# Weight sums with plus signs only, added up by DMAs in DRAM from the heads on; eight of eleven down steps by seven products

## The chip, the cores and the metric

The kernel runs on one core of one Trainium2 chip. The metric is the device time of one execution in microseconds (us); for the kernel before, the median of three runs is 1213.9 us (1212.75 to 1214.02). PE is TensorE (its weight loads are PEld), DVE is VectorE, ACT is ScalarE, POOL is GpSimd, and SP is SyncE, which here only issues DMAs.

## The reference, and what is computed

One layer of a hybrid decoder on 16 meta tokens and 256 tokens, with a model width of 2048, all in float32:

```
u = rmsnorm(h, norm_mix);  proj = u @ w_in           # 2048 -> q, k, v, gates of 8 retention and 4 mLSTM heads
mix = concatenate([ret, hm]) @ w_out                 # the heads' outputs, normed and gated
h = h + mix
u = rmsnorm(h, norm_ffn)
up = causal_dwconv(u @ w_up, ffn_conv_w, ffn_conv_b) # 2048 -> 2 x 5632, convolution over 3 tokens
gate, val = split(up)
h = h + (silu(gate) * val) @ w_down                  # 5632 -> 2048
return rmsnorm(h, norm_final)[:, 16:]
```

## The kernel before, in words

**Products.** Every product of float32 matrices is made of three matmuls: a value is split into a high part (a cast to the type fp32r, by ACT) and a low part (value less high part, by DVE), and high x high, high x low and low x high are summed in PSUM. For weights this is `load_w`: SP loads 512 KB into a buffer `wraw` (four buffers, L118), ACT casts it into `whi` (L121), DVE subtracts into `wlo` (L123; five buffers each). `project` and `half_tile` then issue L130, L131 and L133.

**Stages.** In-projection with the heads (to about 355 us of the profiled span), out-projection (to about 465), and then the FFN in two halves: up stage of half 0 (88 column tiles, `wu`, until 720), down stage of half 0 (720 to 834), up stage of half 1 (to 1089), down stage of half 1 (to 1201), and the last norm and the stores. Each `load_w` serves a half of a product, 1024 weights per partition.

**The down stages.** Each half's part of the hidden width is cut into 11 steps q of 256 rows, and the output's columns are taken in two pairs of blocks, b = 0 and b = 2, each of two times 512 columns. A plain step loads two tiles of `wd` and makes 24 matmuls of N=512 (`product`, L807, L808, L810). A fast step (`seven`) takes the 2 x 2 blocks of activations (A11 to A22, 128 x 128 each) and of weights by seven products in the place of eight, after Strassen and Winograd, so 21 matmuls (L839, L840, L842). For that it needs sums of the activations' blocks (S1 to S4, by POOL, L782 to L785, while the up stage runs) and sums of the weights' blocks. The weights of such steps lie in a DRAM input `wd7`, four pieces of 128x512 for each step.

**The weight sums.** A fast step's raw tile (`raw`, one of two slots `left[0]` and `left[1]` in the array `hT`, which is free by then) takes a sum `kept` in its piece 0 (256 KB, L820) and three pieces of `wd7` (768 KB, L821). DVE then makes two more sums: `ta` (two pieces, 128x1024, L824) and `tb` (128x512, L825), both in `wraw` buffers. ACT casts and DVE subtracts (`split`, L744 and L746) raw[2:4], raw[0:2], ta and tb in this order, one `whi` and `wlo` each, and PE follows. `kept` is made early, in the up stage of the same half: the class `Early` has POOL load three pieces (L715, 768 KB), DVE subtracts and adds (L720, L721), and POOL stores 256 KB in DRAM (L722). A POOL operation on the last gate (`pace`, L713) sets when each of the 26 early loads is issued.

**Which steps are fast.** `FAST` is 1, 2, 3, 5, 6, 7, 8 of the 11. In the last pair of half 1 the last two of them (`BOTH`) are plain, so that the end can be reached column by column; for these, A21 is kept as a split pair `a21`. That makes 7 + 7 + 7 + 5 = 26 fast steps. After a pair, `share` adds the products that several output blocks need, with adding DMAs from POOL's queue into `hn` (`onto`, L858).

**Order.** Each engine takes its instructions in the order in which the scheduler put them, by the code's order and by when operands and buffers are free. SP's queue holds all weight loads of these stages one behind the other, so a load that waits for its buffer holds back those behind it.

Of the kernel before, what the change touches and what calls it, by code (L numbers as in the profile page):

```python
# [34 lines left out]
WARM = 8  # L35

# [47 lines left out]
def trunk(ctx: ExitStack, tc: tile.TileContext, io, out: bass.AP):  # L84
# [28 lines left out]
    last_load = None  # L113

    def load_w(src, shape, to=None):
        nonlocal last_load
        raw = wpool.tile(shape, F32, name="wraw", bufs=4)
        last_load = nc.sync.dma_start(raw, src)  # L118
# [34 lines left out]
    def rsqrt_m2(r0, t, v, n, after):  # L153
# [7 lines left out]
        return r0  # L161

# [43 lines left out]
    with pool("sq", 1, side="right") as sqp:  # L206
        for k0, k1 in [(0, 1), (1, 2)] + [(k, k + 2) for k in range(2, KT, 2)]:
# [4 lines left out]
            raw = wpool.tile([P, 2, W0], F32, name="wraw", bufs=4)[:, :n, :]  # L212
# [405 lines left out]
    pace = midp.tile([P, 1], F32, name="pace")  # L618
# [11 lines left out]
    def conv3(ps, f, name):  # L630
        u = wk2.tile([P, NQ], F32, name="cu")
# [58 lines left out]

    NQD = NHF // 2
    FAST = [1, 2, 3, 5, 6, 7, 8]
    PLAIN = [q for q in range(NQD) if q not in FAST]

    BOTH = FAST[-2:]
# [5 lines left out]
    class Early:  # L704


        def __init__(self, b, q, home, after):

            self.home, self.age = home, 0
            self.kept = dram.tile([P, 512], F32, name=f"kept{b}_{q % NQD}", bufs=1)  # L710

            if after is not None:
                after = nc.gpsimd.tensor_tensor(out=pace, in0=after[:, 0:1], in1=after[:, 0:1], op=ALU.add)  # L713
            with tc.issue_after(after.ins) if after else nullcontext():
                nc.gpsimd.dma_start(home, io["wd7"][b // 2, q][:, 0:3, :])  # L715

        def finish(self, after):
            t = self.home[:, 0, :]
            with tc.issue_after(after.ins):
                nc.vector.tensor_tensor(out=t, in0=self.home[:, 1, :], in1=t, op=ALU.subtract)  # L720
            nc.vector.tensor_tensor(out=t, in0=self.home[:, 2, :], in1=t, op=ALU.add)  # L721
            nc.gpsimd.dma_start(self.kept, t)  # L722

    for half in range(2):
        units = [(b, q) for b in (0, 2) for q in FAST if (half, b) != (1, 2) or q not in BOTH]

        homes = [left[0][:, 0:3, :], left[1][:, 0:3, :], x5[:, 1:4, :]]
        if half == 0:
            begins = [2 + 4 * i for i in range(9)] + [36, 37, 38, 40, 41]
            homes = 9 * [homes[2]] + homes + homes  # L730
        else:
            begins = [2 + 38 * i // (len(units) - 1) for i in range(len(units))]
            homes = 5 * homes
        assert len(begins) == len(units)
        early, running = {}, []

# [4 lines left out]
        a21 = [midp.tile([P, len(BOTH), P], F32R, name=n) for n in ("a21h", "a21l")]  # L741
# [6 lines left out]
        gt = None  # L748
        for jj in range(NHF):
            j = half * NHF + jj  # L750
            pair = []
            for s in range(2):
                pair.append(project(io["wu"][2 * j + s], uh, ul, 0))
                if j == 0 and s == 0:
                    norm2()
                for e in running:
                    e.age += 1
                if running and running[0].age == 2:
                    running.pop(0).finish(evacuated)
                if 2 * jj + s in begins:  # L760
                    n = begins.index(2 * jj + s)
                    b, q = units[n]
                    running.append(Early(b, half * NQD + q, homes[n], gt))
                    early[b, q] = running[-1].kept
# [12 lines left out]
            else:  # L777
                e11, e21, e12, e22 = even[:, 0:P], even[:, P:], gt[:, 0:P], gt[:, P:]
                if half == 1 and q in BOTH:
                    split(*(a[:, BOTH.index(q), :] for a in a21), e21)  # L780
                sums = x_tile(0).rearrange("p (a t) -> p a t", a=4)
                nc.gpsimd.tensor_tensor(out=sums[:, S1, :], in0=e21, in1=e22, op=ALU.add)  # L782
# [266 lines left out]
```

## Time and profile before

| What | us |
|---|---|
| median of 3 runs | 1213.9 |
| lowest and highest run | 1212.75, 1214.02 |
| the profiled execution | 1212.13 |
| its span in the trace | 1210.4 |
| PE busy | 1198.6 |
| DVE busy | 970.1 |
| ACT busy | 708.5 |
| POOL busy | 165.1 |

The time is the whole execution, the span what the trace covers of it. A group's row names line, engine, operation, what is written from what, the shape and the count; then the busy time in us and the mean of one in ns; then the engine's idle time ahead of these instructions, and what ended most of it. A row of waits reads "engine, tile and line, <- who released it: us in total, times, longest". A timeline's row has the start, the duration in us and the instruction; one matmul's duration includes time in PE's pipeline, so what a matmul costs is read from the distance of the starts.

### The profile page before, as it was taken

The numbers are of one execution on the slowest core, as the hardware profiler recorded it, in microseconds if no ns is written. First come the engines' busy times: TensorE is split into PE (matmuls) and PEld (weight loads), VectorE is DVE, ScalarE is ACT, GpSimd is POOL, SyncE is SP. The second block draws the span as 40 slices with busy tenths as digits, with TensorE's granted clock in tenths as the row PEclk, the third lists the DMA queues.
The fourth block names the chain that finished last, engine by engine and source line by source line (L and its number), as shares of the span: only waits on it lengthen the run. The fifth ranks groups of instructions, "written<-read, shape, count | busy, mean of one in ns | idle before, by whom it ended". The sixth has DMA issues, their size and how long they took to land.

```text
span 1210.4 us, 22758 instructions
## 1 busy us (share of the span) xinstructions
PE 1198.6 (99%) x8956; PEld 1155.6 (95%) x8956; DVE 970.1 (80%) x1444; ACT 708.5 (59%) x963; POOL 165.1 (14%) x228
## 2 busy tenths in 40 slices
PE   9999999999999999999999999999999999999997
PEld 9999999999999999999999997788999999998886
DVE  8877778766775767789888879996798778789897
ACT  8657646656556656555555546665555555556674
POOL 0100001111110211021122210202022112100232
PEclk9999999999999999999999999999999999999999
DMA  8765555656564655766766775959777677755956
GB/s 277 265 220 160 166 189 171 199 175 189 181 193 141 208 178 176 248 220 208 246 225 209 270 268 202 261 200 272 275 252 261 216 245 239 259 177 208 286 179 185
DMA packets 83004, 263.27 MB, mean 218 GB/s; under 512 B 14672, under 2 KB 18896, under 8 KB 82768
## 3 DMA queue, kind: packets, MB, share of 16 engines
q1 hardware_dynamic: 71952, 223.85, 56.4%
q0 software_dynamic: 10368, 37.11, 10.0%
q8 instruction: 70, 1.15, 0.4%
q10 hardware_dynamic: 576, 0.85, 0.2%
q14 instruction: 38, 0.31, 0.1%
HBM read 243.42 MB, written 11.27 MB: 210 GB/s over the span
## 4 chain that ended last, share of the span: by engine, by line
PE 92%; DMA 4%; DVE 2%; issue 1%; ACT 0%; SPq 0%; DVEq 0%; POOL 0%; ACTq 0%; POOLq 0%
PE mmps L130 25%; PE mmps L131 25%; PE mmps L133 24%; PE atps L807 3%; PE atps L808 3%; PE atps L810 2%; PE mmps L842 2%; PE mmps L839 1%; PE mmps L840 1%; PE atps L842 1%; PE atps L840 1%; PE atps L839 1%; DMA wraw<-in_wd 1%; DMA hT<-in_wd 1%; DVE wlo L746 1%
## 5 line engine op out<-in xcount | busy, mean ns | idle before, releaser
L121 ACT CAST whi<-wraw 128x1024 fp32r<-128x1024 f32 x352 | 368.7, 1049 | 316.6 <-PE mmps L131 216.9
L123 DVE TENSOR_TENSOR wlo<-wraw,whi 128x1024 fp32r<-128x1024 f32 x352 | 433.1, 1232 | 71.9 <-ACT whi L121 69.6
L130 PE MATMUL mmps<-uh,whi 128*128 128x258 f32 x1408 | 346.7, 283 | 0.0
L131 PE MATMUL mmps<-ul,whi 128*128 128x258 f32 x1408 | 346.6, 283 | 0.0
L131 PEld LDWEIGHTS mmps<-ul,whi 128*128 128x128 f32 x1408 | 266.6, 189 | 0.1
L130 PEld LDWEIGHTS mmps<-uh,whi 128*128 128x128 f32 x1408 | 266.4, 189 | 0.1
L130 PE MATMUL mmps<-xh,whi 128*128 128x272 f32 (+2 forms) x864 | 219.9, 288 | 0.0
L131 PE MATMUL mmps<-xl,whi 128*128 128x272 f32 (+2 forms) x864 | 218.4, 286 | 0.0
L133 PE MATMUL mmps<-uh,wlo 128*128 128x258 f32 x1408 | 199.0, 283 | 0.0
L133 PEld LDWEIGHTS mmps<-uh,wlo 128*128 128x128 f32 x1408 | 181.3, 189 | 0.0
L131 PEld LDWEIGHTS mmps<-xl,whi 128*128 128x128 f32 x864 | 163.0, 189 | 0.0
L130 PEld LDWEIGHTS mmps<-xh,whi 128*128 128x128 f32 x864 | 162.7, 188 | 0.1
L133 PE MATMUL mmps<-xh,wlo 128*128 128x272 f32 (+2 forms) x864 | 126.8, 286 | 0.0
L133 PEld LDWEIGHTS mmps<-xh,wlo 128*128 128x128 f32 x864 | 114.4, 188 | 0.0
L633 DVE TENSOR_TENSOR cu<-mmps,rstd 128x258 f32<-128x258 f32 x88 | 37.3, 424 | 47.6 <-PE mmps L133 47.1
L746 DVE TENSOR_TENSOR wlo<-hT,whi 128x1024 fp32r<-128x1024 f32 x52 | 62.8, 1236 | 5.6 <-ACT whi L744 5.0
L744 ACT CAST whi<-hT 128x1024 fp32r<-128x1024 f32 x52 | 53.3, 1051 | 23.4 <-DMA hT<-in_wd 5.6
L131 PE MATMUL mmps<-mixl,whi 128*128 128x258 f32 x256 | 63.0, 283 | 0.0
L130 PE MATMUL mmps<-mixh,whi 128*128 128x258 f32 x256 | 62.4, 283 | 0.0
L744 ACT CAST whi<-wraw 128x1024 fp32r<-128x1024 f32 (+1 forms) x52 | 42.1, 835 | 18.5 <-DVE wraw L824 4.8
L807 PE MATMUL atps<-whi,mh 128*128 128x512 f32 (+1 forms) x132 | 50.9, 387 | 2.0 <-ACT whi L121 2.0
L746 DVE TENSOR_TENSOR wlo<-wraw,whi 128x1024 fp32r<-128x1024 f32 (+1 forms) x52 | 51.4, 1014 | 0.8 <-PE mmps L842 0.2
(276 smaller groups left out, 1704.4 us busy)
## 6 DMA issues: line engine op xcount, KB each, us to landing
wraw<-in_wu SPq DMA_DIRECT2D x176, 512.0 KB, 4.4
wraw<-in_wi SPq DMA_DIRECT2D x108, 512.0 KB, 4.2
hT<-in_wd SPq DMA_DIRECT2D x26, 768.0 KB, 4.5
wraw<-in_wd SPq DMA_DIRECT2D x36, 512.0 KB, 5.1
wraw<-in_wo SPq DMA_DIRECT2D x32, 512.0 KB, 3.8
x<-in_wd POOLq DMA_DIRECT2D x14, 768.0 KB, 7.6
hT<-in_wd POOLq DMA_DIRECT2D x12, 768.0 KB, 6.4
hn<-x POOLq DMA_DIRECT2D x27, 256.0 KB, 7.8
```

Source lines behind the costliest of these rows:

```text
L121: nc.scalar.copy(hi, raw)
L123: nc.vector.tensor_tensor(out=lo, in0=raw, in1=hi.bitcast(F32), op=ALU.subtract)
L130: nc.tensor.matmul(ps, hi[:, k, :], xh(kk), start=kk == first, stop=False)
L131: nc.tensor.matmul(ps, hi[:, k, :], xl(kk), start=False, stop=False)
L133: nc.tensor.matmul(ps, lo[:, k, :], xh(kk), start=False, stop=kk == last)
L633: evacuated = nc.vector.tensor_tensor(out=u, in0=ps[:, :NQ], in1=rstd2, op=ALU.mult)
L744: copied = nc.scalar.copy(hi, x)
L746: return copied, nc.vector.tensor_tensor(out=lo, in0=x, in1=hi.bitcast(F32), op=ALU.subtract)
L807: nc.tensor.matmul(ps, ah[i], hi[:, i, cols], start=first and i == 0, stop=False)
L808: nc.tensor.matmul(ps, al[i], hi[:, i, cols], start=False, stop=False)
L810: nc.tensor.matmul(ps, ah[i], lo[:, i, cols], start=False, stop=last and i == 1)
L842: nc.tensor.matmul(o, sh[:, f, m, :], lo[:, i, :], start=False, stop=end)
```

## The change

The signs of the sums are turned: S1 is now A21 - A22 and S4 is A12 + S2, and `share` subtracts the other way about. With that, `kept` and `tb` are sums of pieces of `wd7` with plus signs only, and both can be made by DMAs that add.

`Early` keeps two sums in DRAM for each fast step, `kept` of [128, 2, 512]. SP copies two pieces of `wd7` into it, DRAM to DRAM, 512 KB (L203); POOL's queue adds the two other pieces to the first, 256 KB each (L214), and then the first to the second (L216), which is what tb was. Ahead of each adding DMA stands a POOL operation on the high part of the weight tile just cast (L209). The parts are no longer bound to the up stages: they are spread over the loads, the i-th of 116 at load 40 + 38 * i / 16, so from the heads on to load 313.

In `seven`, tb comes by SP from `kept[:, 1]` (L837), and DVE only makes ta (L838). The four `wraw` buffers are now two of `wraw0` and two of `wraw1` (`raw_home`). ta and tb take only `wraw1`, so each has one buffer, and plain loads within a stretch of fast steps take `wraw0`. The load of a plain step behind a fast one is issued ahead of that fast step (`load_plain`).

`FAST` is now 1 to 8, and `BOTH` its last three, so that 8 + 8 + 8 + 5 = 29 steps are fast. `a21` is put in `left[1]` while half 1's up stage runs, and ACT copies it (L905) at the start of the down stage. The buffer of `cu` in `conv3` is single. In the last pair the steps stand in the order 0, 1, 6, 2, 7, 3, 4, 5, 8, 9, 10.

```diff
+    def load_raw(src, shape, side=None):
+        raw = raw_home(shape, loads % 4 // 2 if side is None else side)
...
     def load_w(src, shape, to=None):
-        raw = wpool.tile(shape, F32, name="wraw", bufs=4)
-        last_load = nc.sync.dma_start(raw, src)
+        w = split_w(load_raw(src, shape), shape, to)
+        paced += 1
+        while ahead and ahead[0][0] <= paced:
+            ahead.pop(0)[1](w[0])
+        return w
...
-    FAST = [1, 2, 3, 5, 6, 7, 8]
-    BOTH = FAST[-2:]
+    FAST = [1, 2, 3, 4, 5, 6, 7, 8]
+    BOTH = FAST[-3:]
...
+        def begin(self, hi):
+            with tc.issue_after(last_load.ins):
+                nc.sync.dma_start(self.kept, self.w[:, 1::2, :])
+
+        def add(self, i, hi):
+            t = self.kept[:, 0, :]
+            x = hi[:, 0, 0:1].bitcast(F32)
+            with tc.issue_after(nc.gpsimd.tensor_tensor(out=pace, in0=x, in1=x, op=ALU.add).ins):
+                self.start(i, t)
+
+        def start(self, i, t):
+            if i < 2:
+                nc.gpsimd.dma_start(t, self.w[:, 2 * i, :], accum_op=ALU.add)
+            else:
+                nc.gpsimd.dma_start(self.kept[:, 1, :], t, accum_op=ALU.add)
+    ahead = sorted((4 * n + 3 * i, n, i) for n in range(len(units)) for i in range(4))
+    ahead = [(AHEAD + AHEAD_STEP * i // 16, early[units[n]].parts[p]) for i, (_, n, p) in enumerate(ahead)]
...
-                nc.gpsimd.dma_start(home, io["wd7"][b // 2, q][:, 0:3, :])
-
-        def finish(self, after):
-            t = self.home[:, 0, :]
-            with tc.issue_after(after.ins):
-                nc.vector.tensor_tensor(out=t, in0=self.home[:, 1, :], in1=t, op=ALU.subtract)
-            nc.vector.tensor_tensor(out=t, in0=self.home[:, 2, :], in1=t, op=ALU.add)
-            nc.gpsimd.dma_start(self.kept, t)
...
-            nc.sync.dma_start(raw[:, 0, :], early[b, q])
+            kept = early[b, half * NQD + q].kept
+            nc.sync.dma_start(raw[:, 0, :], kept[:, 0, :])
             nc.sync.dma_start(raw[:, 1:4, :], io["wd7"][b // 2, half * NQD + q][:, 1:4, :])
-            ta, tb = (wpool.tile([P, 2, 512], F32, name="wraw", bufs=4) for _ in range(2))
+            ta, tb = (raw_home([P, 2, 512], 1) for _ in range(2))
+
+            nc.sync.dma_start(tb[:, 0, :], kept[:, 1, :])
             nc.vector.tensor_tensor(out=ta, in0=raw[:, 0:1, :].to_broadcast([P, 2, 512]), in1=raw[:, 1:3, :], op=ALU.subtract)
-            nc.vector.tensor_tensor(out=tb[:, 0, :], in0=raw[:, 3, :], in1=raw[:, 0, :], op=ALU.subtract)
...
+            def load_plain(q):
+                side = 0 if q == plain[0] or q not in steps[steps.index(fast[-1]) + 2 :] else plain.index(q) % 2
+                for j in range(1 if q in alone else 2):
+                    raws[q, j] = load_step(b + j, q, side)
+
+            for n, q in enumerate(steps):
+
+                if q in plain and (q, 0) not in raws:
+                    load_plain(q)
+                if n + 1 < len(steps) and steps[n + 1] in plain and q in fast:
+                    load_plain(steps[n + 1])
```

Below is DVE in the middle of a stretch of fast steps, in half 0's first pair, one step. hT_72 is the raw tile's array, the first `wraw` of a pair is ta, the second tb, and the numbers count tiles. Of before:

```order
L824 TENSOR_TENSOR wraw_9328<-hT_72 128x1024
L825 TENSOR_TENSOR wraw_9329<-hT_72 128x512
L746 TENSOR_TENSOR wlo_9320<-wraw_9286,whi_9319 128x512
L746 TENSOR_TENSOR wlo_9333<-hT_72,whi_9332 128x1024
L746 TENSOR_TENSOR wlo_9343<-hT_72,whi_9342 128x1024
L746 TENSOR_TENSOR wlo_9353<-wraw_9328,whi_9352 128x1024
L746 TENSOR_TENSOR wlo_9363<-wraw_9329,whi_9362 128x512
```

The same place of the changed kernel, where the splits have line L768 and ta has L838; the last row is the next step's first:

```order
L768 TENSOR_TENSOR wlo_9428<-hT_72,whi_9427 128x1024
L838 TENSOR_TENSOR wraw1_9423<-hT_72 128x1024
L768 TENSOR_TENSOR wlo_9438<-hT_72,whi_9437 128x1024
L768 TENSOR_TENSOR wlo_9448<-wraw1_9423,whi_9447 128x1024
L768 TENSOR_TENSOR wlo_9458<-wraw1_9424,whi_9457 128x512
L768 TENSOR_TENSOR wlo_9475<-hT_72,whi_9474 128x1024
```

The subtraction of tb is gone, and ta has moved from ahead of the step's first split to behind it.

Next is SP's queue of DMAs at the end of the first stretch of fast steps of half 0 and in the plain steps behind it, of before; `wraw` 9421 and 9439 are step 9, 9457 and 9475 are step 10, and 9509 is the first of step 0 of the second pair:

```order
L820 DMA hT_72<-kept2_1_8066 128x512
L821 DMA hT_72<-in_wd7 128x1536
L118 DMA wraw_9421<-in_wd 128x1024
L118 DMA wraw_9439<-in_wd 128x1024
L820 DMA hT_72<-kept2_2_8358 128x512
L821 DMA hT_72<-in_wd7 128x1536
L118 DMA wraw_9457<-in_wd 128x1024
L118 DMA wraw_9475<-in_wd 128x1024
L118 DMA wraw_9509<-in_wd 128x1024
```

The same place of the changed kernel, from the load of tb of the first stretch's last step on; kept2_1 and kept2_2 are the sums of the second pair's first two fast steps, `wraw0` 9552 and 9554 are step 10, 9604 and 9606 step 0, and step 9 (9464 and 9466) was loaded further ahead:

```order
L837 DMA wraw1_9471<-kept0_8_87 128x512
L833 DMA hT_72<-kept2_2_89 128x512
L834 DMA hT_72<-in_wd7 128x1536
L837 DMA wraw1_9643<-kept2_1_88 128x512
L126 DMA wraw0_9552<-in_wd 128x1024
L126 DMA wraw0_9554<-in_wd 128x1024
L126 DMA wraw0_9604<-in_wd 128x1024
L126 DMA wraw0_9606<-in_wd 128x1024
```

Each fast step has one DMA more, the one of tb, and it stands behind the two DMAs of the next step's raw tile; step 9's loads have moved ahead of these rows, and the loads of step 10 stand behind tb of the next pair's first fast step.

More of the change, by code (lines that the diff above doesn't have):

```diff
@@ L755, in trunk @@
                     norm2()
[L756 to L764, printed above, removed]
             gt = conv3(pair[0], j, "gt")
@@ L889, in trunk, with load_step, split_step @@
             junk = more.tile([P, 512], F32, name="junk", bufs=1)
-        def load_step(b, q, to=wpool):
-            return load_w(io["wd"][b, half * NQD + q], [P, 2, 512], to)
+            kept21 = more.tile([P, 2, len(BOTH), P], F32R, name="a21", bufs=1)
+            nc.scalar.copy(kept21, left[1].rearrange("p a n -> p (a n)")[:, 0 : 2 * len(BOTH) * P].rearrange("p (s f n) -> p s f n", s=2, n=P))
+            a21 = [kept21[:, s] for s in range(2)]
+        def load_step(b, q, side):
+            return load_raw(io["wd"][b, half * NQD + q], [P, 2, 512], side)
+        def split_step(raw, to=wpool):
+            return split_w(raw, [P, 2, 512], to)
         lag = 4
```

67 lines of the change are left out of this document (33 added, 34 removed).

## The prediction

> **What bounds the kernel now.** I read the page's first lines and its chain first, then the waits, then the stages one by one.
>
> ```profile
> span 1210.4 us, 22758 instructions
> PE 1198.6 (99%) x8956; PEld 1155.6 (95%) x8956; DVE 970.1 (80%) x1444; ACT 708.5 (59%) x963; POOL 165.1 (14%) x228
> PE 92%; DMA 4%; DVE 2%; issue 1%; ACT 0%; SPq 0%; DVEq 0%; POOL 0%; ACTq 0%; POOLq 0%
> ```
>
> PE is busy 1198.6 of 1210.4 us, and the chain that ended last is PE for 92% of the span. What PE waits for, in the whole execution, is three lines:
>
> ```profile
> PE atps L807 <- ACT whi L121: 2.0, 2, 1.3
> PE atps L199 <- DVE ones L173: 1.2, 1, 1.2
> PE atps L130 <- ACT whi L224: 0.2, 1, 0.2
> ```
>
> So the time is PE's matmuls, plus 1.4 us at the start, 2.0 us (two waits) in the down stages, and the tail. An edit gains only by what it takes from PE's instructions or from those two waits; it loses by any new wait. The windows by stage say where a new one is near (columns: length, then busy us of PE, PEld, DVE, ACT and POOL, the granted clock, DMA's share, GB/s): the up stage of half 0, the down stage of half 0, then those of half 1.
>
> ```profile
> 465.00:720.00 255.00, 255.00 (x2116) 254.94 (x2115) 216.71 (x330) 138.82 (x187) 47.02 (x71) 1.00 0.70 235
> 720.00:834.00 114.00, 111.83 (x489) 90.94 (x489) 105.51 (x112) 69.70 (x80) 10.58 (x12) 1.00 0.70 220
> 834.00:1089.00 255.00, 255.00 (x2114) 254.83 (x2113) 199.45 (x298) 139.47 (x188) 40.87 (x68) 1.00 0.74 244
> 1089.00:1201.00 112.00, 112.00 (x511) 92.71 (x510) 101.89 (x110) 71.93 (x93) 24.25 (x23) 1.00 0.68 214
> ```
>
> In the up stages DVE is busy 216.71 of 255 us and has room. In the down stages it is busy 105.51 of 114 and 101.89 of 112 us, 91 to 93%: there it almost keeps step with PE, and there the change is made. The clock is granted in full throughout.
>
> **1. Nine matmuls fewer (gain, on the path).** A fast step is 21 matmuls of N=512, a plain one 24. The fast steps go from 26 to 29, so 3 x 3 = 9 go, and the order's count agrees. Their price:
>
> ```profile
> 827.12 1.99 PE L810 MATMUL atps<-wlo,mh 128*128 128x512 f32 x8
> 828.95 0.39 PE L807 MATMUL atps<-whi,mh 128*128 128x512 f32 x1
> ```
>
> From 827.12 to 828.95 eight matmuls were begun: 0.229 us each. 9 x 0.229 = **-2.06 us**.
>
> **2. The two waits (gain).** Both stand at plain steps that follow seven-product steps in half 0.
>
> ```profile
> 740.76 0.50 PE L807 MATMUL atps<-whi,mh 128*128 128x512 f32 x1 [0.76 <-ACT whi L121]
> 767.04 0.50 PE L807 MATMUL atps<-whi,mh 128*128 128x512 f32 x1 [1.28 <-ACT whi L121]
> ```
>
> The first is step 4, which becomes fast: it goes. The second is step 9, whose loads the new code issues a step early, in buffers that no sum uses: it goes too. 0.76 + 1.28 = **-2.04 us**. What is late next is the step behind it (7, below).
>
> **3. The early subtractions (nothing).** They are 26 x 2 operations on DVE:
>
> ```profile
> L720 DVE TENSOR_TENSOR x<-x 128x512 f32<-128x512 f32 x14 | 9.7, 690 | 10.4 <-DMA x<-in_wd 10.4
> L721 DVE TENSOR_TENSOR hT<-hT 128x512 f32<-128x512 f32 x12 | 8.2, 684 | 0.0
> ```
>
> 26 x (0.690 + 0.684) = 36 us of DVE go, all from the up stages, where PE waits for nothing: they buy 0.
>
> **4. The early DMAs and their pace operations (nothing, 0 to +3).** In the place of 26 loads and 26 stores come 29 copies of 512 KB on SP's queue and 87 adding DMAs on POOL's, each behind a POOL operation that reads a fresh weight tile.
>
> ```profile
> L713 POOL TENSOR_TENSOR pace<-gt 128x1 f32<-128x1 f32 x26 | 19.1, 733 | 135.9 <-DVE gt L768 122.0 <-issue 13.9
> hn<-x POOLq DMA_DIRECT2D x27, 256.0 KB, 7.8
> kept<-hT POOLq DMA_DIRECT2D x12, 256.0 KB, 4.8
> L858 POOL DMA_DIRECT2D hn<-x x27 | 23.8, 960 | 171.6 <-ACT x L864 143.8 <-ACT x L931 14.5 <-DVE x L867 6.2
> ACT whi L121 <- PE mmps L131: 216.9, 173, 4.2
> ```
>
> On POOL that is 87 x (0.73 + 0.96) = 147 us at most, over some 900 us: it was busy 40 to 47 us of each 255. Queued behind a waiting pace operation are POOL's sums for the fast steps and, in the heads, its adds; DVE and ACT wait for those, PE later. A weight tile now also stays until POOL has read it. The cover is ACT's lead: it waited 216.9 us for PE to free a buffer, so it runs ahead of PE as far as its five buffers allow, and a pace operation of 0.73 us fits in a buffer's turn. I take 0. An adding DMA on this queue lands after 7.8 us where a plain one of its size takes 4.8; 87 of them, three times the 27, could disturb the loads. If the cover went for one adding DMA, its extra 3.0 us would stand in PE: bound +3. A gain is excluded, since nothing that PE waits for becomes earlier.
>
> [...]
>
> **5. A fast step on DVE.** Its row sequence before, and in it what goes (L825, the sum tb):
>
> ```profile
> 1117.86 1.22 DVE L824 TENSOR_TENSOR wraw<-hT 128x1024 f32<-128x1024 f32 x1
> 1118.99 0.68 DVE L825 TENSOR_TENSOR wraw<-hT 128x512 f32<-128x512 f32 x1
> 1119.59 1.82 DVE L746 TENSOR_TENSOR wlo<-wraw,whi 128x1024 fp32r<-128x1024 f32 x2
> 1121.33 2.35 DVE L746 TENSOR_TENSOR wlo<-hT,whi 128x1024 fp32r<-128x1024 f32 x2
> 1123.60 1.22 DVE L824 TENSOR_TENSOR wraw<-hT 128x1024 f32<-128x1024 f32 x1
> ```
>
> From L824 to L824 the period is 5.74 us. L825 took 1119.59 - 1118.99 = 0.60 of it, which leaves 5.14. The order now puts ta between the first and the second split, and the third split waits for ta (1.22), ACT's cast of it (1.05) and two handovers: I add 0.1, so 5.24. PE's fast step is 21 x 0.229 = 4.80. DVE still loses 0.44 a step, and now eight steps stand in a row, where seven of them were mixed with four plain steps. Its lead in half 1:
>
> ```profile
> 1089.25 0.24 PE atps L807
> 1095.47 1.22 DVE L746 TENSOR_TENSOR wlo<-hT,whi 128x1024 fp32r<-128x1024 f32 x1 [0.40 <-ACT whi L744]
> ```
>
> The second fast step's first split ended at 1096.69; PE needs it after 24 + 21 matmuls, at 1089.25 + 45 x 0.229 = 1099.55. Lead 2.86, and six more steps use 6 x 0.44 = 2.64. DVE alone just fits.
>
> **6. The loaded tb (loss).** tb now comes by DMA, into the one buffer that the last step's tb left; ta and tb have two buffers of their own and no others. So its load can't be issued until that last tb has been split, and it stands on SP's queue behind the 256 KB and the 768 KB of the next step but one.
>
> ```profile
> 1117.97 0.33 SPq L820 DMA_DIRECT2D hT<-kept  x1
> 1118.34 0.42 SPq L821 DMA_DIRECT2D hT<-in_wd  x1
> hT<-kept SPq DMA_DIRECT2D x26, 256.0 KB, 2.6
> hT<-in_wd SPq DMA_DIRECT2D x26, 768.0 KB, 4.5
> ```
>
> Let X be the end of a step's split of raw[0:2], when the raw tile is free and the raw pieces of the next step but one are issued. From 256 to 768 KB the landing grows by (0.42 + 4.5 - 2.6) / 3 = 0.76 per 256 KB, if three pieces lie between 256 KB alone and the whole megabyte. So the raw is in at X + 4.92 and the next step's tb, behind it, at X + 5.68. When is it asked for? The last two splits of a step take 1121.33 - 1119.59 = 1.74, the last one 0.6 of it; so DVE comes to the next tb at X + 1.74 + 5.24 - 0.6 = X + 6.38, and ACT's cast of it stands ahead:
>
> ```profile
> L744 ACT CAST whi<-wraw 128x512 fp32r<-128x512 f32 x26 | 16.1, 619 | 7.1 <-PE atps L808 2.4 <-PE mmps L840 2.2 <-DVE wlo L746 1.4
> ```
>
> 6.38 - 0.62 - two handovers of 0.1 = X + 5.55. tb is 0.13 late, so a step costs DVE 0.57 more than PE's 4.80, not 0.44: 6 x 0.57 = 3.42. Less the lead of 2.86 that is 0.56 for each of the two stretches that follow an up stage; for the stretch of half 0's second pair, which follows plain steps short of loads, I guess a lead of 2, so 1.4. Sum 0.56 + 0.56 + 1.4 = **+2.5 us**. Bounds: 0, if tb lands within its 2.6; +7.1, if it lands 0.25 later each step (6 x 0.82 = 4.92, so 2.1 + 2.1 + 2.9).
>
> [...]
>
> **7. The passages (loss).** Plain steps 9 and 10 and the next loads behind them (step 0 of the next pair, or the next up stage) stand behind each of three stretches of fast steps. Step 9 is now loaded early; but plain loads have two buffers there where they had four, so step 10 and the step after it wait for a buffer's turn: load, cast, split.
>
> ```profile
> DMA to landing us min/median/max: 3.5/5.5/8.1
> 1130.21 1.05 ACT L121 CAST whi<-wraw 128x1024 fp32r<-128x1024 f32 x1 [2.52 <-DMA wraw<-in_wd]
> L123 DVE TENSOR_TENSOR wlo<-wraw,whi 128x1024 fp32r<-128x1024 f32 x352 | 433.1, 1232 | 71.9 <-ACT whi L121 69.6
> ```
>
> The turn is 3.5 + 1.05 + 1.23 + 0.3 for issue and handovers = 6.1 at the least landing (this row is of 1120 to 1150), against 24 x 0.229 = 5.49 for PE's plain step: 0.6 each, three times, **+1.8 us**. Bounds: 0, if the lead that step 9 gains covers it; 2.6 a passage, +7.8, at the median landing. I stay near the least, since a step's two loads are in flight together and the longer landings hold the time behind the load ahead.
>
> **8. The start of half 1's down stage (loss).** The second fast step's raw tile now holds the halves kept for the last steps, which ACT must copy away first (a new wait of SP's queue; behind it stand tb of the next step and all loads). Below: 0, if step 0's 24 matmuls cover it; above: 1.5, one copy with its handover. I take **+0.5 us**.
>
> **The sum:** -2.06 - 2.04 + 2.5 + 1.8 + 0.5 = +0.7 us. The profiled execution took 1212.13 us (span 1210.4); with the change 1212.8. The median of the three runs shown is 1213.9, 1.8 above that execution, so the forecast as a median is **1214.6 us**. A measurement of this kernel tells about 0.2%, 2.4 us, from no change: the forecast is "the same".
>
> **The rivals.**
> Faster (0.25): the loads land sooner than I take. For it: the least landing is 3.5 and the passages' first load is early; against it, a DMA share of 0.7 in these stages. Then only 1.2 us of new waits are left of 4.8, and -4.1 + 1.2 = -2.9: 1211.0 us.
> Slower, by tb's single buffer (0.23): one mechanism, in the stretches of fast steps; ACT's cast of tb waits for the DMA, DVE's split behind it, and PE at the last three matmuls of every step from the fourth or fifth on. It decides when tb lands later than about 3.4 us after its issue. At 0.25 us a step that is 7.1, with passages of 3 and 0.5 at the start: -4.1 + 10.6 = +6.5, 1220.4 us. For it: the landing of 768 KB is 4.5 median and wd's 512 KB takes up to 8.1; against: 256 KB took 2.6.
> Slower, in the earlier stages (0.07): POOL's queue or the adding DMAs' traffic hold up the heads or the up stages. +3 or more, 1217.6 us. For it: adding DMAs land after 7.8; against: 216.9 us of ACT's waiting for PE.
> That the change doesn't do what it says is excluded by the count of matmuls (954 to 945).
>
> **How the numbers follow.** The forecast has 0.45, faster 0.25, slower 0.23 and 0.07. The range reaches from the faster case, with 0.5 us for the scatter of runs, 1210.5, to the tb case, 1220.5; out of it lie losses over 7 us and a gain of all 4.1. The forecast's own range is 1212 to 1216. Faster by over 0.2%: 0.25; same: 0.45; slower: 0.30.
>
> **What would show each step.** Right: PE's waits list has no wait at step 4 or at step 9; the waits are at L852 to L855, released by ACT's or DVE's tiles of tb, in the last steps of a stretch, and at L819 in steps 10 and 0; the up stages stay at 255 us of PE. Wrong: waits under L130 or L131 in the up stages (4), a wait at the second or third step of a stretch (8, or a lead smaller than 2.86), no waits at all (6 and 7), or a DVE period off 5.24.

## The result, and the profile after

The changed kernel takes 1234.1 us (median of five runs, 1231.6 to 1236.4) where the kernel before takes 1213.9: a ratio of 1.0173, with a 95% interval of 1.0157 to 1.0190. It is 20 us slower; the forecast was 1214.6 with a range to 1220.5. The profiled execution took 1235.55 us (span 1233.8), 23.4 more than that of before (span 1210.4).

The windows of the changed kernel, cut at the same four stages as those of before (length; busy us of PE, PEld, DVE, ACT, POOL; granted clock, DMA's share, GB/s):

```profile
465.00:719.00 254.00, 254.00 (x2117) 253.94 (x2117) 207.35 (x306) 139.75 (x190) 61.09 (x85) 1.00 0.80 231
719.00:845.00 126.00, 117.44 (x487) 90.55 (x486) 101.67 (x102) 71.35 (x84) 12.32 (x14) 0.99 0.75 232
845.00:1098.00 253.00, 253.00 (x2110) 253.00 (x2110) 190.16 (x275) 139.97 (x191) 64.29 (x90) 1.00 0.80 234
1098.00:1226.00 128.00, 119.95 (x516) 93.93 (x514) 101.74 (x108) 72.13 (x95) 21.41 (x23) 0.97 0.68 214
```

The up stages are no longer than before, a little shorter even; PE is still busy there throughout. The down stages, from their first matmul to their last, are 12 and 15 us longer, and there PE now stands idle, though DVE has less to do in them than before (101.67 and 101.74 us in the place of 105.51 and 101.89). The list of PE's waits says for whom:

```profile
PE atps L819 <- ACT whi L140: 8.6, 5, 3.8
PE mmps L852 <- ACT whi L766: 4.0, 8, 0.7
PE mmps L149 <- ACT whi L140: 1.8, 1, 1.8
PE atps L852 <- ACT whi L766: 1.6, 3, 0.7
```

L819 is a plain step and L149 the first product of the next up stage: both stand in the passages, the plain steps and next loads behind each stretch of fast steps. L852 is a fast step. In this kernel L140 and L766 are ACT's casts, L142 and L768 DVE's splits.

**The passages** first. Timelines of the first one, SP's and ACT's:

```profile
767.00 15.38 SPq L126 DMA_DIRECT2D wraw<-in_wd  x5
```

```profile
771.00 1.05 ACT L140 CAST whi<-wraw 128x1024 fp32r<-128x1024 f32 x1 [3.85 <-DMA wraw<-in_wd]
774.01 1.05 ACT L140 CAST whi<-wraw 128x1024 fp32r<-128x1024 f32 x1 [1.97 <-DMA wraw<-in_wd]
779.73 1.04 ACT L140 CAST whi<-wraw 128x1024 fp32r<-128x1024 f32 x1 [3.70 <-DMA wraw<-in_wd]
```

Five plain loads are let go one by one over 15 us, each when a `wraw0` buffer has been split. The two buffers' turns, 771.00 to 779.73, take 8.7 us, in which PE gets one plain step of 5.5 to do. The difference, 3.2, is what PE's matmuls are late in this passage. PE and the clock at that place, and at the passage of half 1:

```profile
777.08 1.10 PE L822 MATMUL atps<-wlo,mh 128*128 128x512 f32 x4
780.83 0.50 PE L819 MATMUL atps<-whi,mh 128*128 128x512 f32 x1 [2.65 <-ACT whi L140]
781.82 0.63 PE L820 MATMUL atps<-whi,ml 128*128 128x512 f32 x1
782.25 0.63 PE L819 MATMUL atps<-whi,mh 128*128 128x512 f32 x1
```

```profile
775.00:785.00 10.00, 7.35 (x24) 5.47 (x24) 4.27 (x4) 5.95 (x10) 3.50 (x4) 0.83 1.01 229
1155.00:1165.00 10.00, 6.11 (x25) 4.67 (x26) 2.71 (x3) 3.55 (x6) 3.74 (x5) 0.93 1.00 229
1165.00:1175.00 10.00, 10.00 (x33) 7.87 (x34) 7.41 (x8) 6.94 (x9) 1.74 (x2) 0.72 0.91 248
```

After a wait of 2.65 us the matmuls start 0.43 apart in the place of 0.23: the granted clock is 0.50 for 3.41 us here, and for 6.82 us at the passage of half 1. The column PEclk (0.83, 0.93, 0.72 of 10 us each) adds up to 5.2 us. But 0.93 of the second window puts the second stretch's begin at about 1163.6, when PE was still waiting (until 1164.76), and half a clock costs nothing there: by the distances of the starts the halved clock cost 4.2 us, after two waits. The prediction has no such term.

**The stretches.** SP's queue and ACT at the end of the first one:

```profile
757.04 0.32 SPq L833 DMA_DIRECT2D hT<-kept  x1
757.41 0.42 SPq L834 DMA_DIRECT2D hT<-in_wd  x1
758.32 0.32 SPq L837 DMA_DIRECT2D wraw<-kept  x1
```

```profile
764.15 0.62 ACT L766 CAST whi<-wraw 128x512 fp32r<-128x512 f32 x1 [1.48 <-DMA wraw<-kept]
```

The raw tile was issued at 757.04, tb at 758.32, and ACT, idle for 1.48 us, got tb at 764.15: 7.1 us after the raw's issue, where the prediction had tb landed at 5.68 and asked for at 5.55. The DMA rows agree (256 KB of tb; the raw's 768 KB took 4.5 before):

```profile
wraw<-kept SPq DMA_DIRECT2D x29, 256.0 KB, 4.7
hT<-in_wd SPq DMA_DIRECT2D x29, 768.0 KB, 5.2
```

**The start of half 1.** The second fast step's raw tile had to wait for ACT's copy of A21 (L905), and SP had issued the third step's raw tile, 1 MB, ahead of it, at 1096.88. Issued from 1099.25 on, it landed at 1108.3, and DVE stood idle for it:

```profile
SPq L833 <- ACT a L905: 1.5, 1, 1.5
```

```profile
1108.39 1.23 DVE L838 TENSOR_TENSOR wraw<-hT 128x1024 f32<-128x1024 f32 x1 [6.01 <-DMA hT<-in_wd]
```

PE waited only 0.9 us at this place. But the lead of 2.86 us with which the prediction let half 1's stretch begin was spent, and that stretch then lost 4.0 us, where the stretches of half 0 lost 1.8 each. No run took the copy away alone.

**The account.** Where two matmuls' starts lie further apart than the matmul's own pace, the excess was added up over PE's timeline, and put down to what is waited for; the second matmul behind a wait starts some 0.10 us late as well (in the kernel before, 767.04 to 767.37), and these are counted apart:

| Term, profiled executions | forecast, us | measured, us |
|---|---|---|
| nine matmuls fewer | -2.06 | -2.1 |
| the waits of before | -2.04 | -2.7, as late starts |
| stretches of fast steps | +2.5 | +8.5, with the start of half 1 |
| passages | +1.8 | +11.4 (3.2, 3.6, 4.6) |
| start of half 1 | +0.5 | 0.9, in the stretches' term |
| halved clock | none | +4.2 |
| second matmul behind a wait, 24 times and 3 before | none | +2.1 |
| pace of the N=512 matmuls | none | +4.2 |
| up stages | 0 | -2.3 |
| sum | +0.7 | 23.3 of 23.4 |

The pace shows in rows like this one, eight matmuls with nothing awaited between them:

```profile
769.85 2.03 PE L822 MATMUL atps<-wlo,mh 128*128 128x512 f32 x8
```

Before, the same eight took 1.99. Less the last one's 0.39 or 0.40, that is 0.2329 each in the place of 0.2286, and so throughout the down stages: 945 x 0.0044 = 4.2 us.

### The profile page after: what moved, and what is told of

The parts are those of the page before. It is cut to its first block, busy times and chain, and to the rows that moved or that the text cites. A ratio compares the mean times of both kernels' runs of the same rounds, so it can differ in the third digit from the quotient of the medians.

```text
span 1233.8 us, 22950 instructions
## 1 busy us (share of the span) xinstructions
PE 1207.8 (98%) x8947; PEld 1152.5 (93%) x8947; DVE 946.9 (77%) x1378; ACT 711.2 (58%) x973; POOL 248.8 (20%) x332
## 4 chain that ended last, share of the span: by engine, by line
PE 88%; DMA 6%; ACT 2%; DVE 2%; issue 1%; SPq 0%; DVEq 0%; ACTq 0%
PE mmps L149 25%; PE mmps L150 25%; PE mmps L152 25%; DMA wraw<-in_wd 2%; DMA wraw<-kept 2%; PE atps L819 1%; PE atps L820 1%; PE atps L822 1%; PE mmps L852 1%; PE mmps L853 1%; ACT whi L766 1%; PE mmps L855 1%; PE atps L852 1%; PE atps L853 1%; PE atps L855 1%
## 5 line engine op out<-in xcount | busy, mean ns | idle before, releaser
L140 ACT CAST whi<-wraw 128x1024 fp32r<-128x1024 f32 x346 | 361.7, 1048 | 356.5 <-PE mmps L150 217.4
L142 DVE TENSOR_TENSOR wlo<-wraw,whi 128x1024 fp32r<-128x1024 f32 x346 | 430.8, 1247 | 107.1 <-ACT whi L140 103.1
L149 PE MATMUL mmps<-uh,whi 128*128 128x258 f32 x1408 | 345.2, 283 | 1.8 <-ACT whi L140 1.8
L149 PEld LDWEIGHTS mmps<-uh,whi 128*128 128x128 f32 x1408 | 265.2, 188 | 2.3 <-ACT whi L140 2.3
L149 PE MATMUL mmps<-xh,whi 128*128 128x272 f32 (+2 forms) x864 | 219.8, 288 | 0.0
L149 PEld LDWEIGHTS mmps<-xh,whi 128*128 128x128 f32 x864 | 162.7, 188 | 0.1
L209 POOL TENSOR_TENSOR pace<-whi 128x1 f32<-128x1 f32 x87 | 51.4, 591 | 415.2 <-ACT whi L140 415.2
L766 ACT CAST whi<-wraw 128x1024 fp32r<-128x1024 f32 (+1 forms) x58 | 47.5, 835 | 51.2 <-DVE wraw L838 23.8
L768 DVE TENSOR_TENSOR wlo<-hT,whi 128x1024 fp32r<-128x1024 f32 x58 | 70.3, 1221 | 5.4 <-ACT whi L766 4.6
L766 ACT CAST whi<-hT 128x1024 fp32r<-128x1024 f32 x58 | 58.7, 1046 | 14.7 <-DMA hT<-in_wd 5.4
L871 POOL DMA_DIRECT2D hn<-x x27 | 23.7, 1012 | 192.5 <-ACT x L878 162.8
L149 PE MATMUL mmps<-mixh,whi 128*128 128x258 f32 x256 | 62.5, 283 | 0.0
```

What stands on the lines that cost most here:

```text
L140: nc.scalar.copy(hi, raw)
L142: nc.vector.tensor_tensor(out=lo, in0=raw, in1=hi.bitcast(F32), op=ALU.subtract)
L149: nc.tensor.matmul(ps, hi[:, k, :], xh(kk), start=kk == first, stop=False)
L209: with tc.issue_after(nc.gpsimd.tensor_tensor(out=pace, in0=x, in1=x, op=ALU.add).ins):
L766: copied = nc.scalar.copy(hi, x)
L768: return copied, nc.vector.tensor_tensor(out=lo, in0=x, in1=hi.bitcast(F32), op=ALU.subtract)
```

## The experiments

Theory: the loads' homes are the cause. Two `wraw0` buffers for the plain loads set the passages, tb's one home sets the stretches, and the halved clock follows from the waits. Rivals: the traffic (adding DMAs into `hn`, early DMAs), and DVE's own pace. All ratios are to the kernel before; intervals are 95%.

**Step 10's loads in the other homes.**

```diff
-side = 0 if q == plain[0] or q not in steps[...] else plain.index(q) % 2
+side = 0 if q == plain[0] or q not in steps[...] else plain.index(q) % 2 if final else 1
```

> The changed kernel, with one thing turned: step 10's two loads take the two wraw1 homes, which lie idle in the passages, and no longer wait for step 9's splits. Theory (homes): in the changed kernel's trace the three passages cost 11.5 us of late matmuls (3.2, 3.6 and 4.6), since a home's turn of load, cast and split takes about 8.5 us for 12 matmuls, and the two waits over 2.6 us are each followed by a stretch of halved clock that costs another 5.1. With four homes in turn the first and the third passage lose at least 6 of their 7.8 us, no wait is over 2.6 us, and the halved clock is gone: 1235.6 goes to 1221 to 1226. Rival (traffic): the loads of the passages are late because of the adding DMAs of the output blocks, whatever their homes: 1231 or more, with waits at the same places. Rival on the clock: the halved clock does not hang on the waits and stays.

Measured: 1224.2 us, 1.0085 (1.0065 to 1.0104), 9.9 us faster than the changed kernel. SP's queue at the first passage now lets four loads go at once, and PE's waits have lost the plain steps:

```profile
763.61 3.64 SPq L126 DMA_DIRECT2D wraw<-in_wd  x4
```

```profile
PE mmps L852 <- ACT whi L766: 4.5, 9, 0.7
PE mmps L149 <- ACT whi L140: 3.2, 1, 3.2
PE atps L852 <- ACT whi L766: 1.8, 2, 1.1
```

The adding DMAs are where they were, so traffic isn't the cause of these waits; the homes are. Nothing is left of the waits before plain steps, and the clock is granted in full from 719 to the end of the matmuls. What stays is one wait of 3.2 us at the second passage, at the first products of the up stage, more than the 2.6 that was expected as the largest; and no halved clock follows it. The stretches' late matmuls rose from 8.5 to 10.0 us.

**tb in two homes.**

```diff
-ta, tb = (raw_home([P, 2, 512], 1) for _ in range(2))
+ta, tb = raw_home([P, 2, 512], 1), x5[:, 4 - 2 * turn : 5 - 2 * turn, :]
```

> The changed kernel, with tb loaded into two pieces of x5 in turn in the place of its one wraw1 home, so that its load no longer waits for a split of the step before. Theory (tb's home): the stretches of fast steps lose 8.5 us of late matmuls in the changed kernel because tb lands 7.0 us after the raw tile's issue where it is asked for after 5.5; with two homes 6 to 7 us of these go, 1235.6 goes to 1228 to 1230, and ACT's waits for wraw<-kept go. Rival (DVE's pace): DVE's own period of over 5.2 us against PE's 4.8 sets the stretches, tb's landing only fills the slack: at most 2 us faster, 1233.5 or more. The passages stay as they are by both.

Measured: 1228.6 us, 1.0118 (1.0100 to 1.0137), 5.5 us faster. ACT's waits for `wraw<-kept` are gone, and in the stretches it now waits for the raw tile:

```profile
ACT whi L766 <- DMA hT<-in_wd: 23.7, 14, 4.9
```

The time is in the expected range, but not by the expected way. The stretches' late matmuls fell from 8.5 to 5.3 us only; the passages gave another 1.8 (from 11.4 to 9.6) and the halved clock 1.1 (from 4.2 to 3.1). So tb's home cost some 3 us of the stretches' 8.5. The other 5.3 stand behind the raw tile and DVE; how they divide between these two is not shown.

**Both.** 

> Both edits: step 10's loads in the wraw1 homes, and tb in two pieces of x5. Theory: what the two give apart adds up, 11 to 14 and 6 to 7 us, so 1214 to 1219, and up to 3 us less if the second passage gains too, since wraw1 then has no tb; if nothing late were left it would be 1208, 4.1 under the kernel before. Rival (traffic and DVE's pace): 1228 or more.

Measured: 1215.8 us, 1.0016 (1.0002 to 1.0029). The two gains, 9.9 and 5.5, add up to 15.4; together they gave 18.3. The three passages have almost no late matmuls left (0.2 us), the stretches 5.4. DVE's rows for ta show its own period, undisturbed:

```profile
806.07 1.22 DVE L838 TENSOR_TENSOR wraw<-hT 128x1024 f32<-128x1024 f32 x1
811.21 1.22 DVE L838 TENSOR_TENSOR wraw<-hT 128x1024 f32<-128x1024 f32 x1
816.36 1.22 DVE L838 TENSOR_TENSOR wraw<-hT 128x1024 f32<-128x1024 f32 x1
```

5.14 and 5.15 us, where the prediction had 5.24. No halved clock is left in this run.

**tb by DVE again**, its load left out.

```diff
-nc.sync.dma_start(tb[:, 0, :], kept[:, 1, :])
+nc.vector.tensor_tensor(out=tb[:, 0, :], in0=raw[:, 3, :], in1=raw[:, 0, :], op=ALU.add)
```

> The changed kernel, with tb made by DVE again (raw[3] + raw[0]) and its load left out; eight fast steps in a row stay. Theory (tb's home): the waits for tb's landing go, but DVE's fast step is 0.6 us longer, 5.84 against PE's 4.80, so eight in a row lose 6 x 1.04 = 6.2 less a lead of 2.9, 3.4 a stretch, 10 us in all in place of 8.5: within 3 us of the changed kernel, 1234 to 1238. Rival (traffic): 256 KB less of each 1.25 MB let the raw tiles and the plain loads land earlier, and it is 3 us or more faster, 1232 or less.

Measured: 1234.6 us, 1.0170 (1.0153 to 1.0186): no change. In the passages some 10.5 of the 11.4 us stayed, though each fast step moves 256 KB less, which again speaks against the traffic. In the stretches 8.8 us are late in the place of 8.5: the 0.6 us on DVE cost about what tb's landing had cost.

**Which address?** All five kernels after the change had the long matmul, 0.233 us, whatever their waits. One thing was common to them: the `pace` tile (4 bytes) lies ahead of the weight buffers, so `whi` and `wlo` begin at 32 modulo 64 bytes of the partition, and before at 0 (addresses as the built programs have them).

```diff
-pace = consts.tile([P, 1], F32, name="pace")
+pace = consts.tile([P, 16], F32, name="pace")[:, 0:1]
```

> The changed kernel, with the pace tile 64 bytes long in the place of 4, so that every buffer behind it, whi and wlo among them, begins at a multiple of 64 bytes of the partition again, as in the kernel before; in the changed kernel they begin 32 bytes off. In the traces a matmul of N=512 takes 0.2333 us in the changed kernel and in all four kernels made from it, and 0.2289 in the kernel before, everywhere in the down stages. Theory (address): the address of the moving operand sets this; the pace goes back to 0.229, which is 945 x 0.0044 = 4.2 us of matmuls, of which the waits in the stretches and passages, set by DVE and DMA, take back a part: 1.5 to 4 us faster than the changed kernel, 1230 to 1232.6 as a median. Rival (load): the pace follows the traffic of the down stages or DVE's share of them, and stays at 0.233: no change, 1233.5 to 1235.

Measured: 1233.6 us, 1.0181 (1.0163 to 1.0200), and the eight matmuls take as long as in the changed kernel:

```profile
768.92 2.03 PE L822 MATMUL atps<-wlo,mh 128*128 128x512 f32 x8
```

The theory as put fell. But in that kernel the activations `mh`, `ml`, `sh` and `sl` had moved too, from 0 to 32.

**The kernel before, moved by 32** (weights and activations both):

```diff
 rstd2 = consts.tile([P, NQ], F32, name="rstd2")
+shift = consts.tile([P, 1], F32, name="shift")
+nc.vector.memset(shift, 0.0)
```

> The kernel before with one more tile of 4 bytes, written once at the start, ahead of the weight buffers, so that they begin 32 bytes off a multiple of 64 as in the changed kernel; nothing else. Theory (address): the pace of the 954 matmuls of N=512 goes from 0.2289 to 0.2333, 4.2 us slower: 1217 to 1219. Rival (load): nothing changes, 1213 to 1214.5.

Measured: 1212.3 us, 0.9995 (0.9983 to 1.0007): no change, against the expectation, and the matmul stays short. In the profiled execution the up stage of half 0 is 1.1 us shorter, and the down stage behind it is 3.3 us longer, by waits; the one at step 9 has grown from 1.28 to 2.51 us.

```profile
773.48 1.99 PE L812 MATMUL atps<-wlo,mh 128*128 128x512 f32 x8
```

**Both homes, all at 64** (with a gap of 32 bytes ahead of `mh`, so that weights and activations both stand at 0):

> Both edits of the homes (step 10's loads in wraw1, tb in x5), and all buffers back at multiples of 64 bytes. Theory: of the 4.2 us of the address at least 2 come out, since few waits are left: 1211.5 to 1214, no slower than the kernel before. If only the waits' edits matter: 1215 to 1216.5 as without the address.

Measured: 1218.2 us, 1.0045 (1.0029 to 1.0061), slower than with the homes alone, though N=512 is at 0.230. The up stages had grown: 255.32 us for the first one in the place of 253.90. That gave the next theory: not where an operand stands counts, but whether weights and activations stand alike.

**All at 32.** With both homes, and then with nothing else but the gap:

```diff
 x5 = midp.tile([P, 5, 512], F32, name="x5")
+midp.tile([P, 8], F32, name="gap")
```

> Both homes' edits, and a gap of 32 bytes ahead of mh, so that the activations of the down stages (mh, ml, sh, sl) begin 32 bytes off a multiple of 64 like whi and wlo, and uh and ul as they did. Behind it stands a new theory of the pace, formed from the eight kernels: N=512 takes 0.2333 where weights and activations differ by 32 bytes in their place (the changed kernel, and the one with 64 bytes alone, where sh had moved), and 0.2289 where they agree (before, before moved by 32, both homes with 64 bytes); and N=258 in the up stages takes 0.1203 where whi and uh differ and 0.1196 where they agree. Then here both are short: 0.229 and 0.1196, the up stages stay 3 us shorter as in the kernel with both homes, and of the 4 us of the down stages the part comes out that the waits don't take: 1212.5 to 1215. Rival (the pace is chance, or of one operand): N=512 stays at 0.233, 1215 to 1216.5.

> The changed kernel, with only the gap of 32 bytes ahead of mh. Theory (weights and activations agree): N=512 at 0.229 in the down stages and N=258 at 0.1196; of 4 us the waits of stretches and passages, which DMA and DVE set, take most: 1230 to 1233. Rival: 0.233, and 1233.5 to 1235.

Measured: 1215.6 us, 1.0018 (1.0005 to 1.0031), and 1230.9 us, 1.0143 (1.0118 to 1.0169). The second one's eight matmuls:

```profile
769.17 2.00 PE L823 MATMUL atps<-wlo,mh 128*128 128x512 f32 x8
```

The pace went as foretold in both. The time of the second did too; that of the first, forecast at 1212.5 to 1215, did not: against the kernel with both homes, 1215.8, nothing can be told, while the stretches' waits grew from 5.4 to 7.8. There PE is not the bound, and a shorter matmul makes a longer wait.

**26 fast steps**, as before, with both homes: first at 64, then at 32 with tb's homes counted from each stretch's start.

```diff
-FAST = [1, 2, 3, 4, 5, 6, 7, 8]
-BOTH = FAST[-3:]
+FAST = [1, 2, 3, 5, 6, 7, 8]
+BOTH = FAST[-2:]
```

> As the kernel with both homes and the 64 bytes, but with the 26 fast steps of before (1, 2, 3, 5, 6, 7, 8, and two fewer in the last pair), so that plain step 4 parts the stretch. It has 9 matmuls more, 2.06 us. Theory (DVE's pace): in the stretches DVE's fast step is 5.14 us against PE's 4.81, so eight in a row leave 5.8 us of waits in the kernel with both homes; a plain step, 5.5 of PE and 2.5 of DVE, gives 3 us of lead back, and most of these go: it is 0 to 3 us faster than with 29, 1209 to 1213. Rival (count): the waits are not DVE's and stay, and it is 2 us slower than with 29.

> As the last, but with the 26 fast steps of before, plain step 4 parting the stretch, and tb's two homes counted from each stretch's start, so that the first tb of a stretch does not take the piece of x5 that an adding DMA still reads (in the earlier kernel with 26 that was 8.3 of its waits). Theory (DVE's pace in eight in a row): the 9 matmuls more cost 2.06, and 3 to 5 us of waits go: 1208.5 to 1212. Rival (the waits aren't DVE's): 2 us slower than with 29, 1215 to 1217.

Measured: 1222.6 us, 1.0095 (1.0077 to 1.0114), and 1217.4 us, 1.0025 (1.0013 to 1.0037). Both missed; the rival's 1215 to 1217 came nearest to the second. The first paid for the borrowed home: in the first down stage SP held the first tb of the second stretch for an adding DMA that still read the piece of x5, PE waited for 3.81 us (until 790.12), and the halved clock followed, with starts 0.43 us apart.

```profile
SPq L838 <- DMA hn<-x: 4.8, 1, 4.8
```

In the second, the down stage of half 0 took 114.2 us against 115.2 with 29 steps, although it has six matmuls (1.4 us) more: some 2.4 us of waits went, so in this stage eight in a row do cost. But the time from the last matmul to the end went from 9.3 to 12.6 us. POOL's last adding DMA there waits for DVE:

```profile
1197.15 0.86 POOL L873 DMA_DIRECT2D hn<-x  x1 [4.09 <-DVE wlo L142]
```

That this wait alone makes the longer tail wasn't tried. No version of the change measured here is faster than the kernel before.

**No early adds.** It leaves out the additions of the weight sums, so its output isn't the layer's.

```diff
-            with tc.issue_after(nc.gpsimd.tensor_tensor(out=pace, in0=x, in1=x, op=ALU.add).ins):
-                self.start(i, t)
+            pass
```

> The changed kernel without the 87 adding DMAs and their 87 POOL operations; the 29 copies stay. It leaves out the additions of the weight sums, so what it computes is not the layer. Theory (cover): in the heads and the up stages PE waits for nothing, so their end stays within 0.5 us (719.2 for the first up stage), and the time within 1 us of the changed kernel, 1233 to 1235. Rival (traffic or POOL's queue): 3 us or more faster.

Measured: 1234.05 us, 1.0155 (1.0131 to 1.0179): no change. The first up stage, 465.05 to 718.95, is as long as with the adds. In these 254 us POOL's busy time fell from 61.09 to 30.32 us and DMA's share from 0.80 to 0.61:

```profile
465.00:719.00 254.00, 254.00 (x2117) 253.94 (x2117) 209.28 (x305) 140.29 (x190) 30.32 (x33) 1.00 0.61 203
```

## Why the prediction was wrong

**Right.** The bound (PE's matmuls), the nine matmuls and the two waits of before came out as forecast. The early subtractions that leave DVE buy nothing, as forecast: with the weights back at 0, the first up stage took 255.32 us without them and 255.04 with them. That 87 adding DMAs and their pace operations cost nothing is shown by leaving them out: 1234.05 us without them, 1234.1 with them. The places of loss were the ones named: the stretches by tb, the passages, the start of half 1. The rival "slower, by tb's single buffer" was the nearest; its 1220 was too low.

**Wrong, step 7, the passages: +1.8 forecast, +11.4 measured.** The mechanism was right and the size was not. The step took the least landing, 3.5 us, since two loads are in flight together; measured landings in the first passage are 3.9 to 6.4. The bound by the median row, 5.5, gave 7.8 us, and it stood in the text as an end that was then not used; it was too low as well, since the turn took 8.7 us in the first passage where that bound has 8.1, and the loads of the last passage took up to 7.5. With step 10's homes turned, 9.9 us go, the halved clock among them, so this step is the largest part of the miss.

**Wrong, step 6, tb: +2.5 forecast, 7.6 measured in the stretches (8.5 with the start of half 1).** Two rows of different DMAs, 256 KB alone and 768 KB behind it, were made into a slope of 0.76 us per 256 KB (the sum as written gives 0.77; the two issues lie 0.37 apart, not 0.42; neither matters); with 1.25 MB in flight tb came 7.1 us after the raw's issue, not 5.68. The step also had the home wrong: tb's load at 758.32 was issued before DVE had split the last tb, when its split of ta ended, since the buffers are handed on in the order in which they come free. And tb is only some 3 us of it: with two homes of its own the stretches still lost 5.3. In half 1 the lead of 2.86 that the step counted on was gone before the stretch began.

**Missing, the halved clock: 4.2, and the slow restarts: 2.1.** A wait was priced at its length. Before, the longest wait of the down stages was 1.28 us, and the clock was granted in full there. In the changed kernel a wait of 2.65 us and one of 3.76 were followed by a granted clock of 0.50, for 3.41 and 6.82 us; so was one of 1.77 in the kernel with tb's two homes, while one of 3.17 in the first experiment was followed by none (last section).

**Missing, the place of the operands: +4.2 in the down stages, -2.3 in the up stages.** A tile of 4 bytes moved the weight buffers behind it. With it the matmul of N=512 went from 0.2286 to 0.2329 us, and the first up stage from 255.04 to 253.90. No row of before could show it, but the address could have been read from the program, and its price only from a run.

**Step 5 held:** DVE's period undisturbed is 5.14, forecast 5.24. The handovers of 0.1 in steps 5 and 6, and the 0.3 for issue and handovers in step 7, were the author's estimates; in the kernel before, at one such place, ACT's cast ended at 1116.68 and DVE's split of it began at 1116.71, 0.03 later. **Step 8** named the right wait, SP's for ACT's copy: 0.9, forecast 0.5; what it left out is the lead that this wait costs the stretch behind it.

## What to carry to other kernels

When buffers are split by use, work out for each place how many homes the loads there have, and compare a home's turn (load at the landing under that traffic, cast, split) with the work that the loads of one turn feed: a turn of 8.7 us on two homes against 5.5 us of work was 3.2 us of late matmuls, whatever the engines' busy shares said. Where a term's bounds lie far apart, take the median row and not the least. A lead that one term counts on can be spent by another. A wait can cost more than its length: here two of PE's, of 2.65 and 3.76 us, cost another 4.2 in halved clock.

## What the runs showed of the hardware

**The pace of N=512 and where the operands begin.** In the seven kernels below, matmuls of N=512 started 0.229 or 0.230 us apart where weights and activations began alike modulo 64 bytes, and 0.233 where they did not. "Weights" are `whi` and `wlo`, "activations" `mh`, `ml`, `sh`, `sl` in the down stages and `uh`, `ul` (always at 32) in the up stages; the places are those where the tiles begin. The pace is the mean distance of starts, of those between 0.222 and 0.240 us; the up stage is the first one, from its first matmul to the first of the down stage.

| Kernel | weights | down: activations | N=512, us | up stage 0, us |
|---|---|---|---|---|
| before | 0 | 0 | 0.229 | 255.04 |
| changed | 32 | 0 | 0.233 | 253.90 |
| changed, 64 | 0 | 32 | 0.233 | 255.32 |
| before, moved by 32 | 32 | 32 | 0.229 | 253.90 |
| both homes, all at 64 | 0 | 0 | 0.230 | 255.32 |
| both homes, all at 32 | 32 | 32 | 0.230 | 253.90 |
| changed, all at 32 | 32 | 32 | 0.230 | 253.90 |

In the down stages both operands were moved, and the pace goes with alike or not in all seven: 0.229 or 0.230 us against 0.233, some 4 ns a matmul. In the up stage only the weights were moved: it is over 1 us shorter with them at 32. Its first row and the first one behind it, in the changed kernel and in the one with 64 bytes, where the stage has the same work:

```profile
465.31 0.28 PE L149 MATMUL mmps<-uh,whi 128*128 128x258 f32 x1
719.21 0.39 PE L819 MATMUL atps<-whi,mh 128*128 128x512 f32 x1
```

```profile
465.08 0.28 PE L149 MATMUL mmps<-uh,whi 128*128 128x258 f32 x1
720.40 0.39 PE L819 MATMUL atps<-whi,mh 128*128 128x512 f32 x1
```

That alikeness decides in the up stage too is not shown, and two things speak against making a rule of it. A row of `uh` has 258 values, 1032 bytes, so in every kernel the rows begin at eight different places modulo 64. And in the in-projection, where the activations' rows have 272 values (1088 bytes, 17 times 64) and begin at 0, a matmul of N=272 took 0.1256 us before, with the weights alike at 0, and 0.1250 in the changed kernel, with them at 32: the other way about. Why it is so, no run here shows; only 0 and 32 were tried.

**The halved clock behind PE's waits.** In the kernel with tb's two homes a wait of 1.77 us was followed by it, with starts 0.43 us apart:

```profile
819.90 0.50 PE L852 MATMUL atps<-whi,sh 128*128 128x512 f32 x1 [1.77 <-ACT whi L766]
820.24 0.67 PE L855 MATMUL mmps<-wlo,sh 128*128 128x512 f32 x2
821.13 0.63 PE L852 MATMUL atps<-whi,sh 128*128 128x512 f32 x1
```

A wait of 2.02 us in the same kernel, until 1126.25, was followed by none. Nor was one of 3.17 in the first experiment (until 845.15), one of 2.32 in the kernel with tb by DVE (784.43) and one of 2.80 in the kernel without the early adds (1166.12), while one of 2.07 (838.10) and one of 2.95 (839.83) in the last two were followed by it. So the length of a wait alone does not tell which.

In the changed kernel the halved stretches inside the stages are 3.41 us long and twice that, and a third one begins behind the last matmul, at 1228.54. Here are the two (columns as above), their starts 382.3 us apart, 112 times 3.413:

```profile
781.39:784.80 3.41, 3.41 (x9) 2.62 (x8) 2.26 (x3) 3.06 (x4) 1.75 (x2) 0.50 0.94 166
1163.69:1170.51 6.82, 5.75 (x14) 4.50 (x15) 4.13 (x4) 5.97 (x8) 1.74 (x2) 0.50 0.85 178
```

Cut into pieces of 3.413 us at these places, this trace has, from 200 us on, three pieces at full clock with PE idle for over 2 us (2.65 from 777.98, 2.7 from 1160.27, and 2.7 from 1225.13, where the matmuls end), and each is followed by halved clock; the next largest, 1.76 from 842.83, is not. In three other traces the places can be estimated from where the starts are 0.43 us apart. The wait of 1.77 then lies within one piece, the one of 2.07 as good as, the one of 2.95 has 2.5 in one; the one of 2.02 that was followed by none lies across two, with some 1.7 and 0.3 in each, the one of 2.32 with 1.4 and 0.9, the one of 2.80 with 1.6 and 1.2. In these four traces it is the idle time within one such piece that goes with the halving, and not the length of the wait. Pieces with 1.76 and 1.77 came out differently; what sets the pieces, and how much idle time it takes, is not shown.

**An adding DMA in DRAM** of 256 KB landed after 6.4 us from the weights and 5.4 from `kept` (medians), between a plain store of that size on the same queue (4.5 and 4.8 before) and an adding DMA into `hn` (7.8 before, 7.2 here). 87 of them cost nothing beside full up stages: 1234.05 us without them, 1234.1 with them, and the first up stage takes 253.90 us in both.
